# Down-projections of the prompt tokens as seven block products, their sums formed in the up stage

## The chip, the cores and the metric

The kernel runs on one core of a Trainium2 chip. A core has a matmul engine (TensorE; PE in the profile, PEld for its weight loads), three engines for element work (VectorE, DVE; ScalarE, ACT; GpSimd, POOL) and a queue engine (SyncE, SP) that issues every DMA of this kernel. The engines run side by side and wait for one another by semaphores. Each takes its instructions in a fixed order: one that waits holds up all that stand behind it. The metric is the time of one execution in microseconds (us).

## The reference

One inference step of a two-layer encoder over 1024 prompt tokens and 8 x 16 sample tokens, width 1024. Every part is computed in single precision.

```python
for l in range(2):
    h = x * (1 + sc_m) + sh_m                 # modulation from c, its own for each request
    mix = attention_l(h) @ w_o                # layer 0: own K/V; layer 1: shared K/V
    x = layer_norm(ALPHA * x + (1 + g_m) * mix)
    h = x * (1 + sc_f) + sh_f
    u = h @ w_up[l]                           # 1024 -> 5632
    y = conv_b + sum(conv_w[t] * shifted(u, t) for t in range(3))
    a, g = split(y)                           # 2816 each
    f = (gelu(g) * a) @ w_down[l]             # 2816 -> 1024
    x = layer_norm(ALPHA * x + (1 + g_f) * f)
    if l == 0:
        k_b, v_b = split((x * (1 + sc_kv) + sh_kv) @ w_kv_b)   # for layer 1
```

The outputs are x and the new K, V and convolution rows.

## The kernel before, in words

All tokens stand in nine tiles of 128: tiles 0 to 7 are the prompt, tile 8 is the sample. A matmul in this kernel reads each operand as two parts, a rounded `hi` and a rest `lo`, and is made of three: lo x hi, hi x lo, hi x hi. Cutting an operand in two is `split`: ACT casts the raw value to `hi` (`copy`, L167), then DVE or POOL subtracts it to make `lo` (L178). So a weight tile costs a DMA, a cast and a subtraction before TensorE may use it. Weights rest in rings of slots (`wslots`, four of 2 x 1024 columns); `subslots` cuts them into halves of 512 columns.

The program runs in stages, layer after layer: attention, output projection (`out_proj`), the up stage (`ffn`) and the down stage (`down`); between the layers `kv` makes layer 1's keys and values.

*Up stage.* The 22 blocks j of 128 hidden columns each have an `a` and a gate part. The first two (`plain`) are ordinary products. The other twenty (`spair`) are made as pairs, `a` block and gate block together, by seven products of half-sized blocks in place of eight (`products`): POOL forms four sums of weights of 128x512 (L1151 to L1154), ACT and DVE split each of the seven, PE does 7 x 24 matmuls of 320 or 256 columns (L1203), and ACT or DVE takes each result out of PSUM and adds it up (L1164, L1171). Then `conv_row` lays the three taps over the rows on ACT and DVE (L1289, L1250), and `gated` applies GELU on ACT, multiplies on POOL (L1297) and stores the block in `actD` (L1298). In layer 0 the modulation matmuls of the coming stages (`ada`, L224) run in the background, one step after every other product.

*Down stage.* Three groups of three tiles, GR = (0,1,2), (6,7,8), (3,4,5). In a group, for each of the 22 blocks j, `fetch` loads the whole weight block (128x1024) and the group's three activation columns (128x384) and splits both, the weights' subtraction on POOL, the activations' on DVE (L1379). `mm` then does 18 matmuls (3 tiles x 2 halves x 3, L1386) into six PSUM banks. So each weight block is loaded and split three times a layer. At a group's end `evict` multiplies the result by the gate (L1399), and `tail` adds the residual and normalizes: in layer 0 by `norm_tail`, which also transposes the rows on PE (L1016), applies layer 1's modulation (L1024 on DVE, L1028 on ACT), splits the result into `H` and stores three copies; in layer 1 by `norm_last`, which writes the output. In the last group the last KEEP blocks are held back and done tile by tile, so that the tiles end one after another.

After layer 0's last tile `kv` begins with nine value tiles (24 matmuls each, L309), then forms the sums of the normalized tiles for its own seven products (`tsums`, L1109 to L1112 and L178), then runs these.

The order of instructions on each engine is made ahead of time by a scheduler that takes the program's order as priority; `issue_after` is a written-out order.

## Time and profile before

| what | us |
|---|---|
| median of 3 runs (2810.69 to 2818.3) | 2810.72 |
| the profiled execution | 2808.31 |
| its span, first to last instruction | 2806.5 |
| matmuls of layer 0's down stage, first to last start | 1050.7 to 1335.9 |
| matmuls of layer 1's down stage, first to last start | 2515.4 to 2791.4 |
| layer 1's up stage, paired blocks | 2059.4 to 2515.3 |

The profiled execution lies 2.4 us under the median. The granted clock was 0.987 of full speed over the span. An instruction's row gives its start, its duration, its engine and line, what it writes and reads, and in brackets how long the engine had been idle and what ended that.

### The profile page before, as it was taken

To read this page: it belongs to the slowest core of one execution; us is meant where nothing else is said; L and a number is where in the kernel's file an instruction comes from. 1 tells how busy PE (TensorE), PEld (TensorE's weight loads), DVE (VectorE), ACT (ScalarE), POOL (GpSimd) and SP (SyncE) were. 2 spreads that over 40 slices of the span, in tenths; PEclk is the share of its full clock that TensorE was granted. 3 is DMA by queue.
4 is the path that set the end of the run, shared out by engine and by line. 5 is a ranking of instruction groups with operands and counts; after the bars stand their busy time and mean duration, and the time that the engine had idled before them with its cause. 6 is when DMAs were issued, how large, how long until landed. Compare 5 with 4: busy or idle time off the path is not lost.

```text
span 2806.5 us, 46569 instructions
## 1 busy us (share of the span) xinstructions
PE 2701.0 (96%) x17398; PEld 2384.3 (85%) x17398; DVE 1898.8 (68%) x3622; ACT 1307.8 (47%) x2607; POOL 1117.7 (40%) x755
## 2 busy tenths in 40 slices
...
GB/s 291 212 157 198 146 98 173 146 250 142 143 156 145 142 132 220 214 225 195 266 199 268 120 153 192 221 202 122 170 123 71 72 80 71 71 143 256 210 199 76
DMA packets 205187, 467.96 MB, mean 167 GB/s; under 512 B 34752, under 2 KB 97936, under 8 KB 204960
## 3 DMA queue, kind: packets, MB, share of 16 engines
...
q8 instruction: 137, 2.24, 0.3%
...
## 4 chain that ended last, share of the span: by engine, by line
PE 40%; DVE 4%; DMA 3%; ACT 2%; issue 1%; POOL 0%; SPq 0%; POOLq 0%; DVEq 0%; ACTq 0%
PE PS L1203 18%; PE PS L1386 10%; PE PS L296 4%; PE PS L309 4%; PE PS L590 1%; PE PS L568 1%; PE PS L540 1%; DVE F L507 1%; DMA F<-hmD 1%; PE PS L543 1%; ACT F L919 1%; PE PS L717 0%; DVE wl L178 0%; DMA F<-hD 0%; DVE xa L178 0%
## 5 line engine op out<-in xcount | busy, mean ns | idle before, releaser
L1203 PE MATMUL PS<-H,wh 128*128 128x320 f32 (+1 forms) x2752 | 427.9, 298 | 0.0
L1203 PEld LDWEIGHTS PS<-H,wh 128*128 128x128 f32 x2752 | 390.3, 192 | 0.4 <-issue 0.4
L1164 DVE TENSOR_TENSOR F<-PS,F 128x256 f32<-128x256 f32 (+1 forms) x446 | 197.7, 453 | 199.7 <-PE PS L1203 198.9
L167 ACT CAST wh<-F 128x512 fp32r<-128x512 f32 (+3 forms) x265 | 168.0, 645 | 328.3 <-PE PS L1203 186.6
L1379 DVE TENSOR_TENSOR xa<-xa 128x384 fp32r<-128x384 f32 x132 | 180.8, 1379 | 190.5 <-ACT xa L167 189.0
L1250 DVE SCALAR_TENSOR_TENSOR F<-F 128x1024 f32<-128x1024 f32 x320 | 258.9, 855 | 4.5 <-ACT F L1289 3.4
L178 DVE TENSOR_TENSOR wl<-F,wh 128x512 fp32r<-128x512 f32 (+2 forms) x236 | 215.0, 924 | 61.9 <-ACT wh L167 61.5
L1203 PE MATMUL PS<-H,wl 128*128 128x320 f32 (+1 forms) x1376 | 244.0, 300 | 8.7 <-ACT F L1171 7.2
L296 PE MATMUL PS<-H,wh 128*128 128x384 f32 (+1 forms) x1152 | 225.1, 339 | 0.0
L1386 PE MATMUL PS<-wh,xa 128*128 128x512 f32 x696 | 222.0, 395 | 0.0
L178 POOL TENSOR_TENSOR wl<-ws,wh 128x1024 fp32r<-128x1024 f32 x59 | 148.6, 2523 | 178.8 <-ACT wh L167 144.1
L1203 PEld LDWEIGHTS PS<-H,wl 128*128 128x128 f32 x1376 | 205.1, 192 | 16.9 <-ACT F L1171 7.7
L1203 PE MATMUL PS<-xa,wh 128*128 128x320 f32 (+1 forms) x1408 | 216.6, 296 | 1.4 <-DVE xa L178 1.4
L167 ACT CAST wh<-ws 128x512 fp32r<-128x512 f32 (+1 forms) x159 | 126.8, 804 | 190.8 <-PE PS L1203 94.8
L296 PEld LDWEIGHTS PS<-H,wh 128*128 128x128 f32 x1152 | 200.9, 189 | 1.3 <-issue 0.8
L1203 PEld LDWEIGHTS PS<-xa,wh 128*128 128x128 f32 x1408 | 197.4, 189 | 2.1 <-DVE xa L178 1.7
L1259 POOL TENSOR_TENSOR F<-F 128x16 f32<-128x16 f32 x88 | 47.8, 543 | 312.4 <-DVE F L1250 220.5
L1386 PEld LDWEIGHTS PS<-wh,xa 128*128 128x128 f32 x696 | 130.6, 188 | 30.7
L167 ACT CAST xa<-xa 128x384 fp32r<-128x384 f32 x132 | 67.4, 513 | 187.6 <-DMA xa<-actD 181.9
L309 PE MATMUL PS<-wh,H 128*128 128x512 f32 (+1 forms) x576 | 145.7, 367 | 1.4 <-DVE F L1095 0.8
L628 POOL TENSOR_TENSOR F<-F,X 64x512 f32<-64x512 f32 x62 | 79.5, 1282 | 169.6 <-DVE F L604 147.7
L1297 POOL TENSOR_TENSOR F<-F 128x1152 f32<-128x1152 f32 x44 | 119.8, 2722 | 49.5 <-DVE F L1250 31.3
...
## 6 DMA issues: line engine op xcount, KB each, us to landing
...
xa<-actD SPq DMA_DIRECT2D x132, 192.0 KB
...
```

Of the source, the lines that this page charges most:

```text
L167: nc.scalar.copy(out, in_)
L178: self.eng(el).tensor_sub(lo, src, hi.bitcast(F32))
L296: mm = self.nc.tensor.matmul(out[:, 0:n], w[a][:, k * 128 : k * 128 + 128], H[:, p, k, s0 : s0 + n], start=i == 0, stop=i == 23)
L309: self.nc.tensor.matmul(out[:, 0:n], H[:, p, j * kn + k, t0 : t0 + 128], w[a][:, k * n : k * n + n], start=i == 0, stop=i == 23,)
L628: self.eng("v" if last else "p").tensor_mul(on[r, q], on[r, q], rb[r, :])
L1164: nc.vector.tensor_add(d, v(ps), a if len(a.shape) == 3 else v(a))
L1203: self.pairmm = nc.tensor.matmul(ps[:, 0:m], w[a][:, k * 128 : k * 128 + 128], x(p, k, n), start=start and c == 0, stop=c == 11, skip_grou ...
L1250: nc.vector.scalar_tensor_tensor(o, u, cw[:, cc, i : i + 1], o, op0=ALU.mult, op1=ALU.add)
L1259: nc.gpsimd.tensor_add(y3[:, :, 0:2], y3[:, :, 0:2], E4[:, cc])
L1297: nc.gpsimd.tensor_mul(yg, yg, ya)
L1379: nc.vector.tensor_sub(lo, raw, hi.bitcast(F32))
L1386: self.downmm = nc.tensor.matmul(ps, a[p][:, i * 128 : i * 128 + 128], w[q][:, hf * 512 : hf * 512 + 512], start=j == 0 and c == 0, stop=j ...
```

## The change

The down-projection of the eight prompt tiles is rewritten as seven products in place of eight. The activations of a block pair m (blocks 2m and 2m+1) are cut by block and by token half into A11 (even block, tokens 0 to 511), A12 (odd, 0 to 511), A21 and A22 (tokens 512 to 1023); the weights by block and by output half into B11, B12 (even), B21, B22 (odd). The numbered products are, summed over the eleven pairs: 1 = A11 B11, 2 = A12 B21, 5 and 6 of two sums each, 3 = sum x B22, 7 = two sums, 4 = A22 x sum. Each is 128x512 by 512 columns for four token tiles: 12 matmuls a pair. The sample tile is not part of it: its matmuls ride along in products 1, 2, 5 and 6, one of 512 columns by 3 a block and half.

- The four weight sums (`weight_sums`) and four activation sums (`act_sums`) of a pair are made on POOL in the up stage, in the blocks with even j (and one at j = 3; the last activation sums fall in the down stage's third step). The weights are loaded into a buffer `w0`, summed in place and stored to `wT`; the activations are summed in place in the two gate buffers and stored to `actS`. Even blocks of `actD` are stored in part only.
- The buffer `w0` is the first of the four weight slots, so in the up stage the products have six half slots instead of eight. The `y` buffers are one for `a` and two for the gate in place of a ring of three.
- In the down stage all splits are on ACT and DVE. The weights' raw halves go through a ring or, in products 3 to 7, directly into the slot.
- Results are combined by ACT copies and DVE additions between products. The residual and the normalization of a tile are in `head`, the rest in `tail`. In layer 0 the sample tile's tail runs in product 3, those of tiles 0 to 3 in product 7, and those of 4 to 7 after product 4. `norm_rows` normalizes on ACT instead of DVE; the modulation of a transposed tile is all on ACT (VA is empty).
- `kv` has become a generator: its first value tiles (0, 1, 2, 3, 8) are issued between the last four tails.

```diff
-VA = (4, 5, 6, 7)
+VA = ()
+NK = NFF // 2
+TAILS = ({1: 8}, {0: 0, 2: 1, 5: 2, 8: 3}, {})
...
-        NW = 4
+        NW = 3
+        self.wslots = [None] + [(wh[:, i], wl[:, i]) for i in range(NW)]
...
-        ys = Ring([F[:, o : o + 1152] for o in (10492, 6396, 7548)])
+        yact = F[:, 10492:11644]
+        ygate = [F[:, o : o + 1152] for o in (6396, 7548)]
...
-            nc.sync.dma_start(self.actD[j], yg)
+            if j % 2:
+                nc.sync.dma_start(self.actD[j], yg)
+                self.pend.append(j // 2)
+            else:
+                for r in (slice(0, 512), slice(1024, 1152)):
+                    nc.sync.dma_start(self.actD[j][:, r], yg[:, r])
+
+        def act_sums():
+            for m in self.pend:
+                a11, a21 = ygate[0][:, 0:512], ygate[0][:, 512:1024]
+                a12, a22 = ygate[1][:, 0:512], ygate[1][:, 512:1024]
+                nc.gpsimd.tensor_add(a22, a21, a22)
+                nc.gpsimd.tensor_sub(a21, a11, a21)
+                nc.gpsimd.tensor_sub(a11, a22, a11)
+                nc.gpsimd.tensor_sub(a12, a12, a11)
+                for i in range(2):
+                    nc.sync.dma_start(self.actS[m, i], ygate[i][:, 0:1024])
+            self.pend = []
+
+        def weight_sums(m):
+            b11, b12, b21, b22 = (t[:, o : o + 512] for t in self.w0 for o in (0, 512))
+            for i in range(2):
+                nc.sync.dma_start(self.w0[i], I["wdn"][l, 2 * m + i])
+            nc.gpsimd.tensor_sub(b11, b12, b11)
+            nc.gpsimd.tensor_sub(b12, b22, b12)
+            nc.gpsimd.tensor_sub(b22, b22, b11)
+            nc.gpsimd.tensor_sub(b21, b22, b21)
+            for i in range(2):
+                nc.sync.dma_start(self.wT[l][m, i], self.w0[i])
...
-        sub = self.subslots(self.wslots)
+        sub = self.subslots(self.wslots[1:4])
...
             def after(i, q):
                 if i % 2 == 0:
                     self.step(1)
+                if i == 1:
+                    act_sums()
+                if i == 2 and j in wsum:
+                    weight_sums(wsum.index(j))
                 if q == 4:
-                    y.append(ys.next())
+                    y.append(ygate[j % 2])
...
+        acts = Ring([(X1[:, o : o + 640], X1[:, o + 640 : o + 1280]) for o in range(0, 8960, 1280)])
+        more = [(H[:, 0, c, 512:1024], H[:, 1, c, 512:1024]) for c in range(8)]
+        def weight(src, ring=None):
+            hi, lo = subs.next()
+            raw = ring.next() if ring else lo.bitcast(F32)
+            nc.sync.dma_start(raw, src)
+            self.split(raw, hi, lo, "a", "v")
+            return hi, lo
...
+        def product(q, banks, bs=None, new=True, keep=0, hook=None):
+            for m in range(NK - keep):
+                a, w, w2 = fetch(q, m)
+                for i in range(4):
+                    mm(self.bank(banks[i]), a, i, w, new and m == 0, m == NK - 1)
+                if bs is not None:
+                    mm(self.bank(bs), a, 4, w2, q in (1, 5) and m == 0, q in (2, 6) and m == NK - 1)
+                if hook:
+                    hook(m)
...
+        product(1, A, 4, hook=start)
+        aff = affs()
+        for i in range(4):
+            nc.scalar.copy(p1[i], self.bank(A[i]))
+        product(2, A, 4, new=False)
+        for i in range(4):
+            gate(c11[i], self.bank(A[i]), i, 0)
+        gate(cs[0], self.bank(4), 8, 0)
+        product(5, B, 4)
+        for i in range(4):
+            nc.scalar.copy(q5[i], self.bank(B[i]))
+        product(6, B, 4, new=False)
+        for i in range(4):
+            nc.vector.tensor_add(u4[i], self.bank(B[i]), p1[i])
+        gate(cs[1], self.bank(4), 8, 1)
...
+        product(3, B, new=False, hook=tails(0))
+        for i in range(4):
+            nc.vector.tensor_add(p1[i], self.bank(B[i]), p1[i])
...
+        product(7, C, hook=tails(1))
+        for i in range(4):
+            nc.vector.tensor_add(u4[i], self.bank(C[i]), u4[i])
+            nc.vector.tensor_sub(q5[i], u4[i], q5[i])
+            gate(u4[i], u4[i], 4 + i, 1)
...
+        product(4, E, keep=keep, hook=tails(2))
+        kept = [(m, fetch(4, m)) for m in range(NK - keep, NK)]
+        for i in range(4):
+            for m, (a, w, _) in kept:
+                mm(self.bank(E[i]), a, i, w, False, m == NK - 1)
+            nc.vector.tensor_sub(q5[i], q5[i], self.bank(E[i]))
+            gate(q5[i], q5[i], 4 + i, 0)
+            if l:
+                tail(4 + i)
+            else:
+                head(4 + i)
+        if not l:
...
+            self.kvrun = self.kv(*ev)
+            next(self.kvrun)
+            for i in range(4):
+                next(self.kvrun)
+                tail(4 + i)
```

292 lines of the change are left out of this document (182 added, 110 removed).

## The prediction

> **What bounds the kernel now.** The page first: its engine shares and the chain that ended last.
>
> ```profile
> span 2806.5 us, 46569 instructions
> PE 2701.0 (96%) x17398; PEld 2384.3 (85%) x17398; DVE 1898.8 (68%) x3622; ACT 1307.8 (47%) x2607; POOL 1117.7 (40%) x755
> ...
> PE 40%; DVE 4%; DMA 3%; ACT 2%; issue 1%; POOL 0%; SPq 0%; POOLq 0%; DVEq 0%; ACTq 0%
> ```
>
> PE is busy 96% of the span and is the largest share of the chain, so a matmul taken away counts in full where PE stands without a gap. Next, the source view of the down matmuls (L1386) in each layer's stretch; columns: line, engine, operation, count, duration in ns, first and last start.
>
> ```profile
> L1386 PE MATMUL PS<-wh,xa x408: 392/394/481, 1050.7 to 1335.9; 128*128 128x512 f32 x136
> ...
> L1386 PE MATMUL PS<-H,xa x540: 392/394/403, 2540.4 to 2766.3; 128*128 128x512 f32 x180
> ...
> L1386 PE MATMUL PS<-wh,xa x288: 392/394/399, 2515.4 to 2788.6; 128*128 128x512 f32 x144
> ...
> L1386 PE MATMUL PS<-xa x216: 387/389/397, 2532.2 to 2791.4; 128*128 128x512 f32 x108
> ...
> L1386 PE MATMUL PS<-wl,xa x144: 392/394/403, 2515.7 to 2788.4; 128*128 128x512 f32 x144
> ```
>
> Layer 1's four groups hold 540+288+216+144 = 1188 matmuls, started from 2515.4 to 2791.4: 276.0 us over 1187 steps, 0.2325 us each. The listed 392 ns is a latency; the spacing is what one costs. Layer 0 takes 285.2 us for as many, with 48 of its tiles' transposes between them.
>
> The third view gives busy time by stretch (PE, PEld, DVE, ACT, POOL, then clock, DMA share, GB/s): ten pairs of layer 1's up stage, the end of layer 0's, the busiest DMA stretch, and layer 1's down stage.
>
> ```profile
> 2133.54:2357.34 223.80, 223.80 (x1682) 223.80 (x1682) 172.81 (x251) 95.04 (x160) 89.65 (x70) 1.00 0.23 75
> ...
> 845.00:1045.00 200.00, 199.91 (x1548) 188.74 (x1546) 142.95 (x210) 82.61 (x137) 88.42 (x61) 1.00 0.41 135
> ...
> 1365.00:1380.00 15.00, 15.00 (x68) 12.43 (x67) 9.62 (x25) 5.47 (x13) 2.77 (x4) 1.00 1.03 399
> 2530.00:2780.00 250.00, 250.00 (x1077) 201.91 (x1076) 139.89 (x153) 103.90 (x146) 156.39 (x61) 1.00 0.61 200
> ```
>
> PE has no gap in either stage, so both are PE-bound. A pair of layer 1 lasts 22.38 us; per pair DVE is idle for (223.80-172.81)/10 = 5.1 us, POOL for 13.4.
>
> **The change, part by part.**
>
> *Fewer matmuls.* Before, 22 blocks x 9 tiles x 2 halves x 3 = 1188 a layer. After, 7 products x 11 block pairs x 4 tiles x 3 = 924, and for the sample tile 22 x 2 x 3 = 132: 1056, all of the same 512 columns. 132 fewer x 0.2325 = 30.7 us a layer, **-61.4 us** in all. All of this stands on PE's path.
>
> *Sums in the up stage.* Each block pair adds eight POOL operations of 128x512 (four on weights, four on activations), all in the even pairs: ten pairs of twenty in a layer. It also adds 3 MB of loads and stores to two pairs. These rows price them (by group; mean ns after the comma):
>
> ```profile
> L1250 DVE SCALAR_TENSOR_TENSOR F<-F 128x1024 f32<-128x1024 f32 x81 | 62.4, 812 | 0.0
> L178 DVE TENSOR_TENSOR wl<-F,wh 128x512 fp32r<-128x512 f32 x50 | 48.5, 970 | 12.0 <-ACT wh L167 12.0
> L1164 DVE TENSOR_TENSOR F<-PS,F 128x256 f32<-128x256 f32 x100 | 44.6, 454 | 36.4 <-PE PS L1203 36.4
> L178 DVE TENSOR_TENSOR wl<-ws,wh 128x512 fp32r<-128x512 f32 x20 | 27.4, 1372 | 2.6 <-ACT wh L167 2.6
> ```
>
> ```profile
> L1297 POOL TENSOR_TENSOR F<-F 128x1152 f32<-128x1152 f32 x10 | 26.9, 2692 | 15.6 <-DVE F L1250 13.8 <-DVE F L1164 1.8
> ...
> L1259 POOL TENSOR_TENSOR F<-F 128x16 f32<-128x16 f32 x20 | 7.7, 383 | 74.6 <-ACT wh L167 38.5 <-DVE F L1250 36.0
> ...
> L1151 POOL TENSOR_TENSOR F<-F 128x512 f32<-128x512 f32 x5 | 6.5, 1292 | 11.1 <-DVE wl L178 11.1
> ```
>
> Eight x 1.29 = 10.3 us, within POOL's idle 13.4. But the engines hinder each other, as the timeline of one pair shows:
>
> ```profile
> 2207.36 2.70 POOL L1297 TENSOR_TENSOR F<-F 128x1152 f32<-128x1152 f32 x1 [1.53 <-DVE F L1250]
> ...
> 2218.37 1.62 POOL L1154 TENSOR_TENSOR ws<-ws,F 128x512 f32<-128x512 f32 x1
> ```
>
> ```profile
> 2205.05 0.68 DVE L178 TENSOR_TENSOR wl<-F,wh 128x512 fp32r<-128x512 f32 x1
> ...
> 2207.86 2.74 DVE L178 TENSOR_TENSOR wl<-F,wh 128x512 fp32r<-128x512 f32 x1
> ...
> 2217.45 1.39 DVE L178 TENSOR_TENSOR wl<-F,wh 128x512 fp32r<-128x512 f32 x1 [0.23 <-ACT wh L167]
> 2218.76 0.48 DVE L1164 TENSOR_TENSOR F<-PS,F 128x320 f32<-128x320 f32 x1
> ```
>
> A split (L178) that takes 0.68 alone took 2.74 when a POOL operation had begun before it, and ended 0.54 after that one (2207.36+2.70 = 2210.06, against 2210.60); POOL's own 1.29 became 1.62 behind a split. The eviction out of PSUM stays at 0.48 beside a running POOL operation. So a DVE operation with both inputs in SBUF and a POOL operation take turns. Now this costs DVE 75.9 - 70 x 0.68 = 28 us in ten pairs, 2.8 us for 8.97 us of POOL work: 0.31 a us. Eight more at that rate cost DVE 3.2 us in an even pair, under the 5.1 idle: hidden on average. Without that cover, each waits its full 1.29: 10.3 - 5.1 = 5.2 late, x10 = 52 us in layer 1. In layer 0 the background's modulation matmuls (L224) share PE:
>
> ```profile
> 845.00:1045.00 200.00, 12.78 (x160) 3.15 (x160) 1.00 0.41 135
> ```
>
> (1548-160)/168 = 8.26 pairs in 200 us: 24.2 each, with DVE idle (200-142.95)/8.26 = 6.9. So 3.4 x 10 = 34 there. Bounds 0 and 86, for both layers. Late evictions bite first (a product is 22.38/7 = 3.2 us, and a bank is read within one), and an even pair's gate buffer must be summed and stored before its conv row may write it: ACT waits there with casts and evictions behind it. The nearest row, 0.31, gives nothing, the burst of taps something: I take 1 us an even pair in layer 1, 0.5 in layer 0: **+15 us**. SP gets seven more issues in two pairs; a store that waits for POOL holds the up-weights queued behind it, whose slots are two pairs deep. The DMA share of 0.23 to 0.41 leaves room, 65 GB/s more beside 75 to 135. Six half slots instead of eight still run 19 us ahead. All three at 0, inside the bounds.
>
> *The streams of the down stage.* Each step's splits go to ACT and DVE (in the old stage POOL took the weights'). A step of 12 matmuls is 2.8 us and needs two DVE splits, 1.4 us, so products without tails are safe; products 5 and 6 need three in 3.5 us. Product 7 carries four tiles' tails. A weight cast and one tail in layer 0 (ACT, then DVE):
>
> ```profile
> 2223.19 0.62 ACT L167 CAST wh<-ws 128x512 fp32r<-128x512 f32 x1 [1.23 <-PE PS L1203]
> ```
>
> ```profile
> 1359.82 1.51 ACT L1028 ACTIVATE F<-PS,C 128x128 f32<-128x128 f32 x4
> 1361.20 1.34 ACT L1032 COPY F<-PS 128x512 f32<-128x512 f32 x2
> 1362.44 1.06 ACT L167 CAST H<-F 128x1024 fp32r<-128x1024 f32 x1
> ```
>
> ```profile
> 1342.97 1.28 DVE L975 BATCH_NORM_STATS2 C<-F 128x6 f32<-128x512 f32 x2
> ...
> 1354.72 1.23 DVE L1040 TENSOR_TENSOR F<-F 128x1024 f32<-128x1024 f32 x1
> ```
>
> ACT now does all eight affine pieces (2 x 1.51), two copies (1.34), the cast (1.06) and the normalizing (about 1.1): 6.5, x4 = 26, and 22 casts x 0.62 = 13.6: 40 us in a product of 132 x 0.2325 = 30.7. DVE: 1.28 + 1.23 + residual 1.2, gate 0.7 and small ones 1.3, estimated by their lengths = 5.7, x4 = 23, and 22 x 0.68 = 15: 38. Both overrun, by 9 and 7; what covers it is the seven activation slots, 19.5 us of PE work whose splits (9.5 of DVE) can be done ahead. Behind it twelve operations of 0.7 form the last sums, 8.2, with no cover left. The tails' DMAs are 4 x 2 MB beside 5.8 MB of operands: 14.2 MB, 461 GB/s, where the row above is full (share 1.03) at 399: 4.9 us over. Bounds 0 and 15; I take **+5**, and +4 in layer 1, whose tails store a quarter as much.
>
> *Layer 0's end.* Before, the value tiles filled PE while three tails ran; they still do, now beside four. The one loss was here, with DVE's first operand sum, DVE's busy time (third figure) and PE's wait:
>
> ```profile
> 1368.67 0.42 DVE L1109 TENSOR_TENSOR F<-F 128x256 f32<-128x256 f32 x1 [2.83 <-DMA hmD<-F]
> ```
>
> ```profile
> 1380.00:1390.00 10.00, 10.00 (x52) 8.64 (x51) 10.00 (x28) 8.34 (x24) 0.00 (x0) 1.00 0.95 323
> 1390.00:1400.00 10.00, 8.57 (x62) 7.98 (x61) 10.00 (x34) 7.71 (x25) 0.00 (x0) 1.00 0.95 338
> ```
>
> ```profile
> 1400.84 2.50 PE L1203 MATMUL PS<-xa,wh 128*128 128x320 f32 x8 [1.39 <-DVE xa L178]
> ```
>
> PE waits for the operand sums, with DVE busy all the time. They began 32.7 us after the last down matmul (1336.0). Their target overlaps the sample gate's place, which the tails now use as a buffer to the last: five value tiles (24 x 0.23 = 5.5 each), three tiles' transposes (some 2.7), and the last tail's ACT work (4) and store (2.5) make 37. Bounds 0 and 10; I take **+4**.
>
> *Layer 1's end.* The last tile's chain:
>
> ```profile
> 2791.12 1.37 DVE L1399 TENSOR_TENSOR F<-PS,F 128x512 f32<-128x512 f32 x2 [2.57 <-PE PS L1386]
> ...
> 2797.96 1.24 ACT L997 ACTIVATE F<-F,C 128x1024 f32<-128x1024 f32 x1 [1.18 <-DVE C L996]
> 2799.28 2.34 POOL L998 TENSOR_TENSOR F<-F 128x1024 f32<-128x1024 f32 x1 [6.93 <-ACT F L997]
> 2801.65 1.23 DVE L999 TENSOR_TENSOR F<-F 128x1024 f32<-128x1024 f32 x1 [3.79 <-POOL F L998]
> ```
>
> Tile 7 ends on DVE with two operations (about 2.5) instead of 5: -2.5; but four tiles come 18 x 0.2325 = 4.2 us apart and need some 5.6 of DVE each (1.4 for the last block, 1.5 for the residual's sums, 1.5 of small ones, 1.2 for the add), up to 5 late. I take 0, bounds -3 and +3.
>
> The sum: -61.4 + 15 + 5 + 4 + 4 + 0 = -33 us, 1.2%. The profiled execution took 2808.3 (span 2806.5), the median is 2810.7: 2808.3 - 33 = 2775, by the median 2778.
>
> **The rivals.**
> 1. *The turns fill up* (slower). The eight sums land in the bursts of taps, even pairs run late, PE waits for evictions. It decides where the mean loss of the 20 even pairs passes (61.4-13)/20 = 2.4 us. At the full bound: -61.4+13+86 = +38, 2848; halfway past the point, 2825. For it: 2.74 for 0.68. Against: 0.31 us a us, and DVE's idle time.
> 2. *Each takes its turn for its whole length.* Per pair DVE's paired-input work is 6.2 + 70 x 0.68/10 = 11.0, POOL's 5.2+2.7+0.8 = 8.6; two pairs and the sums 2 x 19.6 + 10.3 = 49.5, against 44.8 of PE in layer 1 and 48.4 in layer 0: 47 + 11 = 58 us lost, -61.4+58+13 = +10: 2820. Against it: a split ends 0.54 behind POOL's end, not 0.68, so the turns are shorter than the rows. The Trainium skill, SBUF — State Buffer, "Who interferes with whom", states this rule: a vector instruction with two SBUF inputs and a GpSimd one that reads SBUF exclude each other, the first to issue keeping the port for its whole instruction. The trace agrees on the exclusion and not quite on its length.
> 3. *Everything is hidden*: nothing but the matmuls, -61+3: 2752. For it: PE without a gap in both stages today.
> 4. *The tails choke the down stage*: SP waits on tails' stores with fetches behind, products 7 and 4 lose 15 us a layer: -61.4+15+30 = -16: 2794.
>
> **How the numbers follow.** Forecast 0.36; rival 1 0.24; 2 0.12 (half of it within 0.3%, which is 8 us and about what a measurement can tell); 3 0.13; 4 0.15 (0.02 of it within). Faster 0.36+0.13+0.13 = 0.62, same 0.08, slower 0.30. The range reaches down past rival 3, to 2750, and up to 2838, leaving out the worse half of rival 1. The likeliest case alone: 2762 to 2795.
>
> **What would show it.** Down matmuls: 1056 a layer, 0.2325 apart, near 246 us. Up stage: DVE's mean split above 1.08, pairs alternately long and short; wrong if an even pair passes 22.38 + 2.4. Waits of PE in products 7 and 4 beyond 10 us a layer would prove the fourth rival, and a first operand sum later than 40 us the step at layer 0's end.

## The result, and the profile after

The changed kernel takes 2850.36 us (median of four runs, 2845.37 to 2852.07), the kernel before beside it 2813.33: a ratio of 1.0132, with a 95% interval of 1.0113 to 1.0150. It is 1.3% slower; forecast were 2778 us and 1.2% faster. The profiled execution took 2852.07 us, 43.8 more than that of before, at a mean granted clock of 0.971 (before 0.987).

The page after, its span, PE's share and the chain that ended last:

```profile
span 2850.0 us, 47209 instructions
...
PE 2682.3 (94%) x17134; PEld 2359.3 (83%) x17134; DVE 2030.9 (71%) x3850; ACT 1347.1 (47%) x2752; POOL 1109.9 (39%) x808
...
PE 16%; DVE 2%; DMA 2%; issue 1%; ACT 0%; SPq 0%; DVEq 0%; ACTq 0%
```

PE has 264 matmuls fewer, yet it is busy only 19 us less where 61 were to go, because it runs at a lower clock for a part of the time (2701.0 - 61.4 = 2639.6, times 0.987/0.971, is 2683); and it is idle 62 us longer (43.5 of span and 18.7 of its own). DVE has 132 us more of busy time. The source view of the down matmuls in layer 1 shows that the saving itself was made:

```profile
L1465 PE MATMUL PS<-wh,xa x584: 389/394/793, 2570.0 to 2825.9; 128*128 128x512 f32 x195
...
L1465 PE MATMUL PS<-wl,xa x292: 392/399/628, 2571.5 to 2825.6; 128*128 128x512 f32 x146
...
L1465 PE MATMUL PS<-H,xa x180: 389/394/399, 2754.0 to 2829.4; 128*128 128x512 f32 x180
```

584 + 292 + 180 = 1056, as forecast; they take 259.4 us, where 0.2325 apart would be 245.3 (1055 steps). By stage, from the starts of the first and last matmul of each (us; "V" is from the first value tile to the first product of layer 1's keys and values, "kv" those products, "attention" from there to layer 1's first paired block):

| kernel | up, layer 0 | down, layer 0 | V | kv | attention | up, layer 1 | down, layer 1 | after the last matmul | span |
|---|---|---|---|---|---|---|---|---|---|
| before | 508.7 | 285.2 | 51.7 | 96.5 | 575.0 | 456.0 | 275.9 | 15.2 | 2806.5 |
| after | 527.9 | 270.7 | 56.3 | 107.2 | 576.8 | 487.6 | 259.3 | 20.6 | 2850.0 |
| difference | +19.2 | -14.5 | +4.6 | +10.7 | +1.8 | +31.6 | -16.6 | +5.4 | +43.5 |

The up stages lose 50.8 us, and the down stages keep only 31.1 of their 61.4. Where the up stage loses, the windows view shows (length, then busy time of PE, PEld, DVE, ACT, POOL with counts, then granted clock, DMA share, GB/s): the first five pairs of layer 0 are the first row, ten late ones the second; the other three are layer 1's first and second pair and its last fourteen.

```profile
542.91:668.38 125.47, 107.70 (x801) 99.12 (x801) 88.41 (x123) 43.32 (x76) 93.36 (x68) 0.90 0.84 298
...
750.11:1003.69 253.58, 253.32 (x1992) 232.89 (x1989) 176.33 (x261) 98.77 (x165) 138.51 (x99) 1.00 0.49 165
...
2082.01:2117.21 35.20, 25.45 (x169) 25.01 (x170) 30.33 (x49) 14.80 (x29) 30.96 (x25) 0.85 0.69 238
2117.21:2142.33 25.12, 22.81 (x171) 22.35 (x170) 24.44 (x26) 9.15 (x16) 23.09 (x15) 1.00 0.55 188
...
2255.43:2569.62 314.19, 313.90 (x2354) 313.41 (x2352) 268.95 (x353) 133.51 (x229) 175.35 (x120) 1.00 0.29 101
```

The last fourteen pairs of layer 1 take 314.19 / 14 = 22.44 us each, though every second has its four activation sums: those cost nothing. The whole loss stands in the first pairs, which last 35.2, 25.1, 30.1, 28.7, 26.9 and 27.5 (before: 29.6 and then 22.4), with DVE and POOL busy nearly throughout. The source view of the first weight sum says why:

```profile
L1347 POOL TENSOR_TENSOR w0f<-w0f x11: 1288/1737/3177, 2064.8 to 2237.2; 128x512 f32<-128x512 f32 x11
```

All eleven weight sums of layer 1 start within 172 us, one in every pair and some pairs with two, instead of one in every second pair over 440. They depend on nothing but their buffer and their loads, so the scheduler puts them as early as the buffer allows, whatever block of the program they are written in. Groups of DVE, each of one shape, and then of POOL in these six pairs (2082 to 2255 us; busy time, mean ns, idle before):

```profile
L1276 DVE SCALAR_TENSOR_TENSOR F<-F 128x1024 f32<-128x1024 f32 x21 | 41.4, 1973 | 0.9 <-ACT F L1315 0.9
L188 DVE TENSOR_TENSOR wl<-F,wh 128x512 fp32r<-128x512 f32 x31 | 45.4, 1469 | 7.1 <-ACT wh L177 6.0 <-issue 0.9
```

```profile
L1348 POOL TENSOR_TENSOR w0f<-w0f 128x512 f32<-128x512 f32 x10 | 18.7, 1866 | 3.7 <-DMA w0f<-in_wdn_dram 3.7
...
L1350 POOL TENSOR_TENSOR w0f<-w0f 128x512 f32<-128x512 f32 x10 | 14.7, 1473 | 0.4
```

The kernel before has, for the same tap of 1024 columns in ten pairs of this stage (the row of the prediction, 812 ns, mixes it with short ones):

```profile
L1250 DVE SCALAR_TENSOR_TENSOR F<-F 128x1024 f32<-128x1024 f32 x41 | 52.4, 1278 | 0.0
```

A split takes 1469 ns in place of 970, a tap of 1024 columns 1973 in place of 1278: beside POOL operations both are longer. PE's waits in the up stage of layer 1 (time, count, longest) then fall on the evictions that stand behind those on DVE and ACT:

```profile
PE PS L1228 <- DVE F L1189: 19.3, 10, 4.8
...
PE PS L1228 <- ACT F L1196: 7.7, 1, 7.7
```

### The profile page after: what moved, and what is told of

Same layout as the page of the kernel before. It is cut to its first block, busy times and chain, and to the rows that moved or that the text cites. A ratio compares the mean times of both kernels' runs of the same rounds, so it can differ in the third digit from the quotient of the medians.

```text
span 2850.0 us, 47209 instructions
## 1 busy us (share of the span) xinstructions
PE 2682.3 (94%) x17134; PEld 2359.3 (83%) x17134; DVE 2030.9 (71%) x3850; ACT 1347.1 (47%) x2752; POOL 1109.9 (39%) x808
## 5 line engine op out<-in xcount | busy, mean ns | idle before, releaser
L1228 PE MATMUL PS<-H,wh 128*128 128x256 f32 (+1 forms) x2624 | 408.9, 298 | 0.0
L1465 PE MATMUL PS<-wh,xa 128*128 128x512 f32 x1144 | 370.2, 402 | 14.8 <-DVE F L1583 5.8
L1228 PEld LDWEIGHTS PS<-H,wh 128*128 128x128 f32 x2624 | 373.6, 192 | 0.0
L1276 DVE SCALAR_TENSOR_TENSOR F<-F 128x1024 f32<-128x1024 f32 x320 | 309.6, 1014 | 27.8 <-ACT F L1315 27.6
L1189 DVE TENSOR_TENSOR F<-PS,F 128x320 f32<-128x320 f32 (+1 forms) x446 | 196.5, 451 | 126.4 <-PE PS L1228 124.4
L188 DVE TENSOR_TENSOR wl<-F,wh 128x512 fp32r<-128x512 f32 (+2 forms) x234 | 245.0, 1056 | 57.4 <-ACT wh L177 55.3
L177 ACT CAST wh<-F 128x512 fp32r<-128x512 f32 (+2 forms) x234 | 137.2, 595 | 314.0 <-PE PS L1228 191.8
L1228 PE MATMUL PS<-H,wl 128*128 128x256 f32 (+1 forms) x1312 | 234.3, 301 | 21.2 <-ACT F L1196 15.2
L1465 PE MATMUL PS<-wl,xa 128*128 128x512 f32 x572 | 229.0, 401 | 0.2
L188 DVE TENSOR_TENSOR xa<-xa 128x640 fp32r<-128x640 f32 (+1 forms) x154 | 124.0, 810 | 119.5 <-ACT xa L177 111.6
L177 ACT CAST xa<-xa 128x640 fp32r<-128x640 f32 (+1 forms) x154 | 104.1, 682 | 169.4 <-DMA xa<-actD 109.5
L188 DVE TENSOR_TENSOR wl<-ws,wh 128x512 fp32r<-128x512 f32 (+1 forms) x149 | 156.1, 1052 | 10.2 <-ACT wh L177 10.2
L1315 ACT ACTIVATE F<-F 128x1152 f32<-128x1152 f32 x80 | 108.0, 1351 | 115.8 <-DVE F L1189 60.1
L1228 PE MATMUL PS<-xa,wl 128*128 128x320 f32 (+1 forms) x664 | 123.4, 308 | 20.8 <-DVE F L1189 20.0
## 6 DMA issues: line engine op xcount, KB each, us to landing
xa<-actS SPq DMA_DIRECT2D x88, 256.0 KB
```

The lines of the kernel that those rows point to most:

```text
L177: nc.scalar.copy(out, in_)
L188: self.eng(el).tensor_sub(lo, src, hi.bitcast(F32))
L1189: nc.vector.tensor_add(d, v(ps), a if len(a.shape) == 3 else v(a))
L1228: self.pairmm = nc.tensor.matmul(ps[:, 0:m], w[a][:, k * 128 : k * 128 + 128], x(p, k, n), start=start and c == 0, stop=c == 11, skip_grou ...
L1276: nc.vector.scalar_tensor_tensor(o, u, cw[:, cc, i : i + 1], o, op0=ALU.mult, op1=ALU.add)
L1315: nc.scalar.activation(y, u[:, 2:1154], AF.Identity, bias=cw[:, cc, 3:4], scale=cw[:, cc, 2:3])
```

## The experiments

The theory at the start: rival 1, made worse by the bunching; the turns of POOL and DVE are the loss, so sums that are spread, moved or left out give it back. Its rival: the loss comes from what lies around the sums, the DMA traffic, one buffer less, the waits in the down stage and the tails. Each ratio is against the kernel before in runs on the same chip; the four without an interval are of one run each. The stages come from one profiled execution of each.

| run | median, us | before there | ratio (95%) |
|---|---|---|---|
| e1_spread_even | 2825.45 | 2806.22 | 1.0068 (1.0046 to 1.0091) |
| e2_spread_odd | 2838.61 | 2806.22 | 1.0107 (1.0083 to 1.0131) |
| e3_no_weight_adds | 2812.00 | 2806.22 | 1.0021 |
| e4_h_split_dve | 2856.52 | 2806.22 | 1.0179 |
| e5_three_places | 2822.55 | 2802.30 | 1.0069 (1.0048 to 1.0091) |
| e6_adds_on_vector | 2840.38 | 2802.30 | 1.0140 (1.0119 to 1.0160) |
| e7_sums_in_layer0 | 2843.10 | 2803.82 | 1.0130 (1.0106 to 1.0154) |
| e8_rows_on_vector | 2843.27 | 2803.82 | 1.0139 (1.0106 to 1.0172) |
| e9_one_per_pair | 2830.09 | 2807.53 | 1.0090 (1.0073 to 1.0107) |
| e10_scale_on_vector | 2823.01 | 2805.21 | 1.0063 |
| e11_tails_first | 2819.19 | 2805.21 | 1.0050 |
| e12_sums_in_attention | 2844.18 | 2806.86 | 1.0136 (1.0115 to 1.0158) |
| e13_one_per_head | 2823.93 | 2806.61 | 1.0057 (1.0043 to 1.0072) |
| e14_three_splits | 2818.24 | 2806.61 | 1.0051 (1.0030 to 1.0072) |
| e15_best_places | 2818.81 | 2804.46 | 1.0059 (1.0038 to 1.0081) |
| e16_copies_first | 2799.97 | 2805.45 | 0.9977 (0.9964 to 0.9990) |

Their stages, as above:

| kernel | up, layer 0 | down, layer 0 | V | kv | attention | up, layer 1 | down, layer 1 | after the last matmul | span |
|---|---|---|---|---|---|---|---|---|---|
| e1 | 520.6 | 264.8 | 56.3 | 107.5 | 574.6 | 477.9 | 257.2 | 21.4 | 2821.9 |
| e2 | 522.2 | 264.6 | 56.1 | 106.9 | 576.2 | 480.9 | 256.5 | 20.3 | 2837.8 |
| e3 | 522.0 | 263.3 | 56.2 | 107.4 | 575.5 | 464.5 | 256.7 | 18.9 | 2810.2 |
| e4 | 528.1 | 259.4 | 63.2 | 111.3 | 580.6 | 489.6 | 255.7 | 19.6 | 2854.6 |
| e5 | 517.2 | 264.5 | 59.7 | 102.6 | 578.5 | 480.1 | 256.0 | 19.4 | 2823.0 |
| e6 | 523.4 | 263.1 | 67.3 | 104.1 | 576.0 | 484.4 | 258.6 | 18.6 | 2835.4 |
| e7 | 549.7 | 265.8 | 62.0 | 111.7 | 575.6 | 460.7 | 260.9 | 18.7 | 2848.6 |
| e8 | 551.7 | 263.5 | 63.5 | 108.0 | 578.5 | 461.4 | 258.4 | 17.3 | 2842.3 |
| e9 | 527.3 | 264.8 | 61.8 | 106.1 | 579.6 | 468.1 | 259.2 | 18.5 | 2824.3 |
| e10 | 520.8 | 264.8 | 56.5 | 104.7 | 578.2 | 474.6 | 257.5 | 19.2 | 2821.2 |
| e11 | 521.1 | 267.3 | 54.5 | 103.9 | 577.2 | 475.0 | 255.8 | 19.8 | 2817.4 |
| e12 | 513.5 | 266.1 | 54.5 | 103.2 | 616.1 | 461.2 | 258.9 | 17.4 | 2829.3 |
| e13 | 512.7 | 269.4 | 54.5 | 103.2 | 601.9 | 461.2 | 257.0 | 16.8 | 2819.7 |
| e14 | 513.1 | 264.2 | 61.6 | 105.7 | 596.4 | 461.3 | 257.9 | 16.4 | 2816.1 |
| e15 | 513.4 | 270.0 | 54.5 | 104.6 | 576.2 | 474.5 | 262.7 | 18.2 | 2815.9 |
| e16 | 516.1 | 262.5 | 54.5 | 103.6 | 577.7 | 477.2 | 252.4 | 17.2 | 2807.1 |

### The weight sums' place and their turns

**e1_spread_even** holds the sums' loads behind the up weights of their pair, and their POOL operations behind the last gated product:

```diff
-            for i in range(2):
-                nc.sync.dma_start(self.w0[i], I["wdn"][l, 2 * m + i])
-            nc.gpsimd.tensor_sub(b11, b12, b11)
+            with self.tc.issue_after(self.wupdma):
+                for i in range(2):
+                    nc.sync.dma_start(self.w0[i], I["wdn"][l, 2 * m + i])
+            with self.tc.issue_after(self.gmul):
+                nc.gpsimd.tensor_sub(b11, b12, b11)
...
```

> The weight sums are tied to their pair: the loads behind that pair's up-weights, the four POOL operations behind the gate product of the pair before; eight sums then stand in each even pair, as the prediction had assumed, and the amount of work is the same. Theory A (the loss of the up stages, 19 and 32 us, comes from the weight sums standing bunched in the first pairs): both stages come back to 2 us a pair or less over the kernel before, 508.7+10 and 456+10 at most, and the whole to 2800 to 2822. Rival B (POOL's added work costs its turns wherever it stands): both stages stay where they are, 528 and 488, and the whole at 2840 to 2855.

**e2_spread_odd** does the same in pair 2 and the odd pairs, where no activation sums stand:

```diff
-        wsum = [2, 3] + list(range(4, NFF - 1, 2))
+        wsum = [2] + list(range(3, NFF, 2))
```

> As the run before, but the weight sums stand in the odd pairs and the activation sums in the even ones: four added POOL operations in each pair. Theory A: the stages within 3 us of the kernel before (512 and 459), the whole 2798 to 2810. Rival B: no change, 2840 to 2855. If the eight in one pair are a cost of their own, this run is 10 us or more under the one with eight in even pairs; if not, the two agree within 4 us.

**e3_no_weight_adds** keeps the loads and stores, bunched as in the changed kernel:

```diff
-            nc.gpsimd.tensor_sub(b11, b12, b11)
-            nc.gpsimd.tensor_sub(b12, b22, b12)
-            nc.gpsimd.tensor_sub(b22, b22, b11)
-            nc.gpsimd.tensor_sub(b21, b22, b21)
```

> The four POOL operations of the weight sums are left out (the products then take the plain weights, so the output is another); the loads of the down weights and the stores stay bunched at the stage's start. Theory A: the stages lose their POOL part, 509 to 515 and 456 to 462, the whole 2798 to 2812. Rival C (the transfers, or the queue that issues them, hold up the up weights): the stages stay near 528 and 488, the whole 2840 or more.

Without the 88 operations of the weight sums the kernel stands 0.2% above before instead of 1.3%: they are most of the loss. What is left of the up stage's loss in e3 (13.3 and 8.5 us) stands in the first four pairs. In layer 0 the sums' loads and stores crowd there (below); in layer 1 some 5 us remain even in e7 and e12, which have none of them in that stage. Spreading the sums gives back a little more than half of their cost. The source view of e1 in layer 1, and two of its neighbouring pairs in the windows view:

```profile
L1349 POOL TENSOR_TENSOR w0f<-w0f x11: 1721/1742/1754, 2086.3 to 2506.3; 128x512 f32<-128x512 f32 x11
```

```profile
2191.09:2214.91 23.82, 22.64 (x171) 22.37 (x170) 21.83 (x26) 10.50 (x17) 15.12 (x12) 1.00 0.39 127
2214.91:2237.28 22.37, 22.37 (x171) 22.37 (x169) 20.39 (x25) 8.15 (x15) 18.00 (x12) 1.00 0.40 142
```

and one of the kernel before:

```profile
2200.00:2222.40 22.40, 22.40 (x171) 22.40 (x170) 17.28 (x26) 9.51 (x16) 8.97 (x7) 1.00 0.24 74
```

Spread, one weight sum costs a pair of layer 1 1.4 us; in layer 0 the pairs behind the first three stay at 25.1 to 25.4, as before, until the background ends. For two pairs POOL's listed time grows by 15.12 + 18.00 - 2 x 8.97 = 15.2 us and DVE's by 21.83 + 20.39 - 2 x 17.28 = 7.7: half a microsecond a microsecond, where the prediction carried over 0.31. The pair with both kinds of sums leaves DVE 2 us idle in 23.8, and its evictions come late. In the odd pairs (e2) it is no better: there nearly every pair of layer 1 takes 22.9 or 23.4, and 5.7 us pass between layer 0's up and down stage.

**e5_three_places** is e1 with layer 0's sums moved away from the stage's first pairs (and two edits for the layer's end, below):

```diff
+        wsum = [2, 3] + list(range(4, NFF - 1, 2)) if l else list(range(6, NFF - 1, 2)) + [11, 15, 19]
```

> The kernel with the weight sums spread over the even pairs, and three edits in three separate stages. (1) Layer 0's weight sums start four pairs later (pairs 6, 8 ... 20 and 11, 15, 19), so that none lies beside the sixteen 384 KB copies of the skew table in pairs 2 to 4. If these copies and the sums' transfers crowd each other out, pair 3 of layer 0 (34.9 us when spread) falls to 29 to 31 us and layer 0's products from 520.6 to 510 to 515 us. If it is the activation sums or the six half slots, pair 3 stays at 33 us or more, the products at 518 us or more. (2) At layer 0's end the norm tails of tiles 4 to 7 use another second buffer, so that the operand sums' region is no longer held by the last stores of h. If that region makes them late, the first operand sum comes 36 to 41 us after the last down matmul (48 now), the first key/value pair takes 27 to 31 us (37.7) and V tiles to first product 51 to 54 us (56.3). If the amount of VectorE and GpSimd work is the limit, they stay at 44, 35 and 55 us or more. (3) In layer 1's last four tiles VectorE makes scale and shift for all four (GpSimd had them for two). If GpSimd's long multiplications block VectorE there, the time from last matmul to end falls from 21.4 to 16 to 18.5 us; if VectorE's own backlog is the limit, it is 21 to 24 us. Together by the first theories 2800 to 2808 us, ratio 0.997 to 1.001; by the others 2822 to 2828 us.

**e6_adds_on_vector** puts the weight sums of e5 on DVE (and, in the down stage, holds back casts and splits and takes the residual part of the tails of tiles 8 and 0 to 3 to DVE, as e7 to e9 also do; below):

```diff
-            with self.tc.issue_after(self.gmul):
-                nc.gpsimd.tensor_sub(b11, b12, b11)
+            nc.vector.tensor_sub(b11, b12, b11)
...
```

> As the kernel with three edits, and four more. (1) The four operations of each weight sum run on VectorE, not GpSimd. VectorE was busy 17.3 us of a pair's 22.4 us before, so 4 x 0.68 = 2.7 us more fit: if the sums cost by the taking of turns, even pairs of layer 1 go from 23.8 to 22.4 to 22.8 us and its products from 478 to 461 to 468 us. If VectorE's total is the limit, they stay at 23.5 and 474 us or more. (2) ScalarE's casts of product 2 from its fourth block on stand behind the copies of product 1's sums, VectorE's splits of product 3 likewise behind the additions after product 6. If the order on these queues makes the boundary stalls, each boundary loses under 1 us (4 to 5 us now): 6 to 8 us less in each down stage. If the banks themselves must be emptied first, 2 us or more stay at each. (3) The norm tails of tiles 8 and 0 to 3 make their residual split on VectorE, those of 4 to 7 on GpSimd as now. By turns, layer 0's products 3, 7 and 4 lose 6 to 10 us less (264.8 us for the stage becomes 248 to 254 with the boundaries), and the V tiles don't pay for it (the run with all nine on VectorE paid 7 us there). If VectorE's total is the limit, the stage stays at 257 us or more. (4) Seven blocks, not six, are kept for layer 1's last tiles: 1 to 2 us less behind the last matmul if a backlog is left there, none if not. Together by the first theories 2760 to 2778 us, ratio 0.983 to 0.989; by the others 2800 us or more.

In both a spare buffer of the last tails lies over the row that scales the normalized rows of layer 0's tiles 4 to 7, so that these rows, which are layer 1's residual, are other numbers; the instructions are the same. Layer 0's second pair (j = 3) in the windows view, in e1 and then in e5:

```profile
572.32:607.18 34.86, 25.52 (x204) 23.27 (x200) 26.33 (x34) 12.11 (x21) 19.11 (x14) 0.96 1.00 369
```

```profile
576.66:604.04 27.38, 25.50 (x204) 23.23 (x201) 16.94 (x26) 8.42 (x15) 8.98 (x8) 1.00 0.97 350
```

The DMA engines are full here in both. A sum in this pair costs 7.5 us, where one in the pairs from 6 to 18 costs nothing (the one in pair 20, behind the background, costs 3.5). In e3, which has the sums' loads and stores here but none of their operations, the pair takes 36.7 us:

```profile
579.60:616.30 36.70, 25.64 (x202) 23.30 (x201) 24.13 (x34) 12.09 (x20) 16.40 (x11) 0.94 1.01 357
```

At this one place it is the transfers, which the prediction had put at nothing. On DVE the sums cost layer 1 4.3 us more than on POOL (484.4 against 480.1, one profile of each): DVE does not take them for less. ACT was not tried.

**e7_sums_in_layer0** puts all 22 weight sums in layer 0's up stage, two in each even pair from 6 to 18 and one in each odd pair from 5 on, where the background matmuls give each pair 3 us more:

```diff
+        wsum = {}
+        if l == 0:
+            for n, j in enumerate(range(6, 20, 2)):
+                wsum[j, 2], wsum[j, 5] = (0, n), (1, n)
+            for n, j in enumerate((5, 7, 9, 11, 13, 15, 17, 19)):
+                wsum[j, 2] = (n % 2, 7 + n // 2)
```

> All 22 weight sums, layer 1's too, are formed in layer 0's up stage (pairs 5 to 19, one in an odd pair, two in an even one), where a pair lasts 25.4 us because background matmuls lie in it and where a spread sum has cost nothing so far. Layer 1's up stage forms activation sums alone. Beside it: at layer 0's end tiles 4 to 7 use a second buffer for h that no operand sum and no normalisation row needs; tiles 8 and 0 to 3 split on VectorE; layer 1's last four tiles scale and shift on VectorE, with seven blocks kept. Theory: the price of a weight sum is the price of the pair it lies in. Then layer 0's pairs stay at 25.1 to 25.8 us and its products at 515 to 521 us (two sums a pair fit), layer 1's products fall from 478 to 458 to 464 us (456.0 before), layer 0's down stage takes 255 to 258 us, the first key/value pair 29 to 34 us with the first operand sum 38 to 43 us after the last down matmul, the last stretch 18 to 19 us. Sum: 2780 to 2796 us beside 2802 to 2807 of the kernel before, ratio 0.991 to 0.998. Rival: a sum costs 1.4 us wherever it lies as soon as GpSimd is full; then layer 0's even pairs take 27 to 29 us, its products 530 us or more, and the whole is 2800 us or more. If the activation sums or the six half slots cost in layer 1, its products stay above 468 us.

**e9_one_per_pair** does at most one in a pair, eleven and four in layer 0 and seven in layer 1:

```diff
+        if l == 0:
+            wsum = {j: (0, j - 5) if j < 16 else (1, j - 16) for j in range(5, 20)}
+        else:
+            wsum = {j: (1, 4 + n) for n, j in enumerate((4, 6, 8, 10, 12, 14, 16))}
```

> From the kernel with the sums spread over even pairs. (1) One weight sum in each of layer 0's pairs 5 to 19 (its own eleven, four of layer 1), the other seven of layer 1 in even pairs of its own up stage. Theory: a pair of layer 0 takes one sum free, not two. Its pairs 5 to 19 stay at 25.1 to 25.8 us, its products at 514 to 521 us, layer 1's at 466 to 472 us (seven at 1.4 us on 461). Rival: odd pairs have no room beside the activation sums; then 525 us or more. (2) Gate, normalisation and first residual rows are loaded in products 2 and 5, not at product 1's end, where transfers kept the DMA engines 91 to 98% busy. If that makes the stall between products 1 and 2, product 2 takes 38.5 to 39.5 us in both layers (43 to 46 in most runs); if it is the copies' place on ScalarE's queue, 42 or more. VectorE's splits of product 3 from its third block on stand behind the additions after product 6: product 6 falls from 44 to 46 us to 39 to 42 if their order is the cause. (3) In tiles 4 to 7 of layer 0 VectorE makes four of the eight scalings of h, as before the change; among the V tiles ScalarE was 84 to 93% busy, VectorE 19 to 38%. If ScalarE is the limit there, V tiles to first product take 52 to 54.5 us (56.3), the first key/value pair 28 to 34 (37.7); if not, 56 and 37 or more. Tiles 8 and 0 to 3 split on VectorE; layer 1's end as in the last runs (17 to 19 us). Together 2776 to 2792 us beside 2802 to 2807, ratio 0.989 to 0.996; by the rivals 2805 us or more.

Nineteen pairs of layer 1 in e7, in the windows view:

```profile
2139.57:2568.84 429.27, 427.11 (x3193) 425.43 (x3192) 364.71 (x478) 180.47 (x309) 237.10 (x164) 1.00 0.27 96
```

22.6 us each, with the activation sums still there: without weight sums layer 1's up stage loses 4.7 us instead of 31.6, which shows their cost by itself. But layer 0 pays more than that (549.7, 41 above before): its pairs in which the operations of two sums ran go up to 31.1 (its profiled execution is the highest of its six). One in every pair (e9) still lengthens some of them, up to 27.8; one in about every second pair (e5) does not.

**e12_sums_in_attention** moves layer 1's weight sums into its attention, and **e13_one_per_head** puts each behind the bias load of a head, with six buffers for the probabilities in place of four, but one weight slot for q in place of two:

```diff
+            if l and 6 <= i < 50 and i % 4 == 2:
+                self.next_weight_sums(i // 4 - 1)
             scores(x)
```

> The kernel with tails first, and layer 1's eleven weight sums formed during layer 1's attention, where GpSimd is busy 6 to 12 us of 50 and the DMA engines 42 to 77%; their buffer is the weight slot w0, for which attention's two weight slots move up by one and two of its six buffers for transposed probabilities go. Layer 0's sums in its pairs 5 to 19, eleven of them; layer 1's end as in the last runs. Theory: the sums cost by the turns that they force on VectorE in a stage where it has no slack, so in attention they cost nothing: layer 1's products take 459 to 463 us (475.0 with tails first, 456.0 before the change), the stretch from the last key/value product to layer 1's first product 575 to 580 us (577.2), layer 0's products 515 to 519 us, the last stretch 18 to 19 us. Together 2794 to 2802 us beside 2802 to 2807 of the kernel before, ratio 0.995 to 0.999. Rival: attention has no room either (the two buffers less, or the turns beside its softmax); then the stretch takes 590 us or more and the whole 2812 us or more.

```diff
-        for i in range(2):
-            nc.sync.dma_start(w[i], self.I["wdn"][1, 2 * m + i])
+        with self.tc.issue_after(self.biasdma):
+            for i in range(2):
+                nc.sync.dma_start(w[i], self.I["wdn"][1, 2 * m + i])
```

> As the run with layer 1's weight sums in attention, but one sum behind the bias load of each of eleven heads (they ran there all eleven in the first 170 us, with the DMA engines 76 to 92% busy), and with all six buffers for transposed probabilities (that run had four, which fall to be written again before they are read, so that its attention's numbers are others) and one weight slot for q. Theory: bunching is again what cost 39 us there; spread, the sums cost nothing in a stage in which GpSimd and the DMA engines have room: the stretch from the last key/value product to layer 1's first product 575 to 584 us (577.2 with the sums in the up stage, 616.1 bunched), layer 1's products 459 to 463 us, layer 0's 512 to 516 us; together 2786 to 2800 us beside 2802 to 2807 of the kernel before, ratio 0.992 to 0.999. Rival: GpSimd's turns cost VectorE in attention as well, or the single q slot does; then the stretch takes 590 us or more and the whole 2808 us or more.

In e12 the four buffers are overwritten before they are read, so that layer 1's attention computes other numbers; its profiled execution is the lowest of its five. PE's waits in the attention of e13:

```profile
PE PS L551 <- DVE C L518: 7.0, 7, 4.8
...
PE PS L601 <- DVE C L736: 6.9, 1, 6.9
```

The same 50 us of layer 1's attention in e11, without the sums, and in e12 (windows):

```profile
1550.00:1600.00 50.00, 45.44 (x280) 40.74 (x279) 32.04 (x97) 32.50 (x76) 10.10 (x14) 1.00 0.42 117
```

```profile
1550.00:1600.00 50.00, 46.06 (x261) 39.73 (x260) 30.40 (x91) 30.37 (x70) 22.12 (x20) 0.95 0.76 222
```

POOL is mostly free there (10.10 of 50 us), but PE waits for small results of DVE, and beside the sums it gets through 261 matmuls in place of 280. Against e11 attention is 39 us longer with bunched sums, 25 with one a head. But turns between POOL and DVE are not what these traces show. The sums of e13 run at their short length, and DVE is listed as busy for 391.2 us of its attention, against 390.4 in e11. The wait of 6.9 us above goes back to ACT, which stood for 8.5 us at a cast into the sums' buffer until a store of the sums had left it:

```profile
L1089 POOL TENSOR_TENSOR w0f<-w0f x11: 1282/1287/1297, 1542.0 to 1777.8; 128x512 f32<-128x512 f32 x11
```

```profile
1788.88 1.04 ACT L177 CAST w0r<-ws 128x1024 fp32r<-128x1024 f32 x1 [8.54 <-DMA wT<-w0f]
```

The wait of 4.8 us goes back, over DVE and POOL, to the load of a head's bias. So the buffer, q's one slot and the transfers (DMA share 0.67 in e13's attention, 0.59 in e11's) are left as causes here, and which of them makes how much of the 25 us stays open. Nothing tried makes the sums free in layer 1.

### Layer 0's end

**e4_h_split_dve** takes the residual part of the transposed tiles from POOL to DVE in all nine tails of layer 0:

```diff
-EL = "p"
+EL = "v"
```

> The changed kernel with the subtraction that splits a normalized tile in layer 0's down stage on DVE instead of POOL, nothing else. If the turns between the engines cost layer 0's last products and the first pair of the key products (39.5 us in product 4 against 30.7, 37.1 in the key pair against 27.0), the two lose 3 to 10 us together and the whole is 2840 to 2847; if DVE's own amount of work is the limit there, it is the same or slower, 2850 to 2856.

Product 4 of layer 0 in the windows view, in the changed kernel and in e14, which does so for four tiles (8, 0, 1 and 2):

```profile
1302.00:1341.50 39.50, 35.28 (x156) 28.05 (x155) 37.69 (x45) 24.44 (x53) 22.00 (x7) 0.96 0.63 227
```

```profile
1283.70:1316.30 32.60, 32.54 (x148) 26.04 (x147) 32.15 (x43) 20.80 (x42) 10.73 (x3) 1.00 0.74 262
```

With these splits on POOL, DVE is busy 37.69 of 39.50 us and product 4 is 7 us longer. Off POOL that is gone, but the value tiles behind it pay the same (63.2 and 61.6 us in place of 56.3 and 54.5). **e14_three_splits** is e13 with that edit; it is not to be told from e13 (1.0051 against 1.0057).

> As the run with one sum per head, and the residual split of tiles 8, 0, 1 and 2 (not 3 to 7) on VectorE. GpSimd's split of 2.4 us and its turns cost layer 0's product 4 some 7 us (39.5 us against 32.4 in each run that had tiles 8 and 0 to 3 on VectorE), but there the V tiles paid 5 us. If tile 3's split alone, the last before the V tiles, made them pay, product 4 takes 33 to 36 us and the V tiles stay at 54 to 55.5 us: 3 to 6 us less than that run, 2782 to 2796 us, ratio 0.990 to 0.998. If every operation more on VectorE before the V tiles is paid there, the V tiles take 57 us or more and the whole is the same within 2 us.

The first 40 us behind the last down matmul, and where the operand sums of the next products begin (windows; timeline):

```profile
1341.50:1381.50 40.00, 39.11 (x185) 31.98 (x185) 25.00 (x53) 26.46 (x52) 17.06 (x7) 1.00 0.68 258
...
1384.96 1.26 DVE L1065 TENSOR_TENSOR F<-F 128x1024 f32<-128x1024 f32 x1 [4.70 <-POOL F L1064]
...
1389.69 1.09 DVE L1134 TENSOR_TENSOR F<-F 128x256 f32<-128x256 f32 x3 [2.50 <-DMA hD<-F]
```

The kernel before has, in the same place:

```profile
1335.90:1375.90 40.00, 40.00 (x190) 33.35 (x189) 27.92 (x51) 16.91 (x35) 15.97 (x11) 1.00 0.64 236
```

The first sum comes at 1389.7 - 1341.5 = 48.2 us (before 32.7; forecast 37), and PE's first pair of products behind it takes 37.1 us in place of 27.0. No engine is full here: each tail goes from ACT to DVE to POOL and back, and the engines wait for one another, as DVE's 4.70 us for a multiplication on POOL show. Is it the buffer over which the sums are formed, as the prediction had it? e5 frees it, by its second edit:

```diff
+            rings = Ring([zt]), Ring([self.hf, self.lng])
```

```profile
L1134 DVE TENSOR_TENSOR F<-F x9: 399/413/1880, 1334.6 to 1403.1; 128x256 f32<-128x256 f32 x9
```

The sums then begin at 8.3 us behind the last down matmul, but those of the last tile at 76.8 (76.5 in the changed kernel): the last tile is the limit, and not the buffer. (e7 and e8 free it as well, with another spare buffer, and begin at 13 us.) **e8_rows_on_vector** is e7 with the residual's multiplication of tiles 4 to 7 on DVE, **e10_scale_on_vector** is e1 with half of the scalings of these tiles on DVE (and five buffers more for raw weights), **e11_tails_first** is e1 with each tail ahead of a value tile:

```diff
-                self.norm_tail(t, row, xdst, aff, True, tb, "a", "pv", None, ...
+                self.norm_tail(t, row, xdst, aff, True, tb, "a", "vv" if t in (4, 5, 6, 7) else "pv", None, ...
```

> As the run with all weight sums in layer 0's up stage, and in the norm tails of tiles 4 to 7 of layer 0 the multiplication of the residual row by the scale row (1024 elements, about 2.6 us on GpSimd) is VectorE's. If VectorE, idle for some 30 us of the V tiles, waits there for GpSimd, the stretch from the V tiles to the first product and the first key/value pair lose 2 to 6 us less together. If VectorE's amount of work is the limit (four more operations of 1.2 us), they lose 2 to 5 us more, as with the split on VectorE (7 and 4 us more). The other stages stay within 1 us of that run.

```diff
-        early = Ring(raws + [F[:, o : o + 512] for o in (0, 512, 1024)])
+        early = Ring(raws + [F[:, o : o + 512] for o in range(0, 4096, 512)])
...
-                self.norm_tail(t, ..., rings[1], EL, VA, self.hD, True)
+                self.norm_tail(t, ..., rings[1], EL, (4, 5, 6, 7) if t in (4, 5, 6, 7) else VA, self.hD, True)
```

> The kernel with the sums spread over even pairs, with two edits alone. (1) At layer 0's end, for tiles 4 to 7 only, VectorE makes four of the eight scalings of h (ScalarE makes all eight in the kernel of the change); the residual split stays on GpSimd. ScalarE is busy 37.9 of the 40 us after the last down matmul there (25.5 before the change), VectorE 28.0. If ScalarE's amount of work is what delays the operand sums, the last of them ends 66 to 72 us after the last down matmul (76.8), the first product starts at 53 to 55 (56.5) and the first key/value pair takes 28 to 33 us (37.7). If VectorE is the limit, as the two runs say that gave it the split or the rows, they come at 77 or more, 56.5 or more and 37 or more. (2) The ring of raw weight halves for products 1 and 2 has fourteen buffers instead of nine, so that the load queue does not stand still until VectorE has split an old one (it stood 6.7 us in product 1). If that standstill makes the stall between products 1 and 2, product 2 takes 38.5 to 39.5 us in both layers (39.3 and 42.5 in the spread kernel, 43.0 and 43.0 in the kernel of the change); if not, layer 1's stays above 42.

```diff
             for i in range(4):
-                next(self.kvrun)
                 tail(4 + i)
+                next(self.kvrun)
```

> The kernel with the sums spread over even pairs; at layer 0's end the norm tail of tiles 4 to 7 stands ahead of a V tile in TensorE's order and not behind it, so that each tile's transposes come some 5.5 us earlier, and the chain transposes, eight scalings, two copies, cast and store with them. If the order (GpSimd waited 12.6 us for the first transposes) makes the operand sums late, the last operand sum comes 71 to 73 us after the last down matmul (76.8) and the first pair takes 32 to 34 us (37.7). If the norms before the transposes are late anyway, TensorE waits for them: the V tiles take 2 to 6 us more, 58 to 62 us, and the last sum stays at 76 or more.

The expectation of e10 counts overlapping instructions twice: the row above has ACT at 26.46 us of 40, not 37.9. Moving its scalings gives 2.8 us in kv, and the sums start no earlier (48.0). e8 is e7 within their intervals. The order of the tails (e11) gives 1.8 in V and 3.6 in kv, and e12, e13, e15 and e16, which have it too, keep that. The rest, some 10 us, was not removed by anything tried here.

### The products of the down stage

From the starts of their matmuls, each product in the changed kernel (us; 165 matmuls 0.2325 apart are 38.4, 132 are 30.7; layer 0 has transposes besides):

| product | 1 | 2 | 5 | 6 | 3 | 7 | 4 |
|---|---|---|---|---|---|---|---|
| layer 0 | 39.0 | 43.0 | 38.5 | 44.5 | 34.5 | 31.7 | 39.5 |
| layer 1 | 39.2 | 43.0 | 38.7 | 44.6 | 32.4 | 30.8 | 30.6 |

The fourth rival's products, 7 and 4, lose nothing in layer 1. Products 2 and 6 lose 4.6 and 6 us in both layers. Product 6 loses about half of them at its end, where PE waits 2.8 us in layer 0 (first row) and 3.0 in layer 1 for the first addition that empties its banks. At the start of product 2 in layer 0 the waits, the timeline and the windows view show:

```profile
PE PS L1465 <- DVE F L1583: 2.8, 1, 2.8
PE PS L1465 <- DVE xa L188: 2.7, 1, 2.7
```

```profile
1113.21 0.72 ACT L177 CAST xa<-xa 128x640 fp32r<-128x640 f32 x1 [7.26 <-DMA xa<-actD]
```

```profile
1111.00:1114.70 3.70, 1.15 (x5) 0.57 (x4) 0.74 (x1) 1.49 (x3) 0.00 (x0) 1.00 1.00 356
1115.57:1118.98 3.41, 3.41 (x10) 2.64 (x9) 2.05 (x3) 3.18 (x6) 0.00 (x0) 0.50 0.46 139
```

ACT stands for 7.26 us before a cast that waits for its load. Behind that cast on its queue stand the four copies that empty product 1's banks, into which product 2 must write; PE idles for 2.55 us and soon after runs 3.41 us at half the clock, which together cost 2.55 + 3.41 x 0.5 = 4.3 of the 4.6 us. The profile has PE's wait end with DVE's split behind that cast (2.7 us, and 2.9 in layer 1), so in the changed kernel the late load ends it, with the copies just behind. Two theories: the transfers are too late (e9 moves three groups of other loads out of the way, e10 has a deeper ring), or the copies stand in the wrong place on ACT's queue. Neither of the transfers' edits helps by itself: product 2 takes 47.7 and 44.4 us in the two layers of e9 and 40.8 and 42.3 in e10, against 39.3 and 42.5 in e1. (It varies: without any edit to it, it takes 38.5 and 40.0 in e5.) **e15_best_places** gathers the best places so far: e11, e12's places in layer 0, the loads moved as in e9, the ring of e10.

> The cheapest places found, in one kernel: layer 0's weight sums as in the last two runs (its products 513 us), layer 1's in the even pairs of its own up stage (475), tails first (V tiles 54.5, key/value stage 103.5), layer 1's end on VectorE (17 to 18.5), all splits of the tails on GpSimd. By these rows: 2817.4 - 8 - 2 = 2807 us. New in it are two edits of product 1's transfers together, which did not help one by one: gate, normalisation and residual rows are loaded in products 2 and 5, and fourteen raw buffers instead of nine keep the load queue from standing. If bytes and a standing queue together make the stall between products 1 and 2, product 2 takes 38.5 to 39.5 us in both layers (40.1 to 47.7 in the runs before) and the whole is 2796 to 2802 us beside 2802 to 2807, ratio 0.996 to 1.000. If the copies' place on ScalarE's queue or the latency of the small sample loads makes it, product 2 stays at 40 us or more and the whole at 2804 to 2812 us.

Product 2 takes 43.1 and 44.4 us there, and now PE waits for the copies (2.8 us in layer 0, first row; 3.8 in layer 1). The timeline in layer 1, just ahead of product 2:

```profile
PE PS L1467 <- ACT x2f L1579: 2.8, 1, 2.8
```

```profile
2580.59 0.72 ACT L177 CAST xa<-xa 128x640 fp32r<-128x640 f32 x1 [3.84 <-DMA xa<-actD]
2581.22 1.55 ACT L1579 COPY x2f<-PS 128x512 f32<-128x512 f32 x3
```

In e6 the order was tried for product 2. In layer 0 it took 38.5 us, but product 5 then 42.5; in layer 1 the copies stood behind the residual's scaling, which waits for its own load:

```profile
2602.24 1.06 ACT L1533 ACTIVATE F<-F 128x1024 f32<-128x1024 f32 x1 [8.20 <-DMA F<-xd]
2603.20 2.03 ACT L1577 COPY x2f<-PS 128x512 f32<-128x512 f32 x4
```

**e16_copies_first** is e15 with the order alone changed: from the fourth block on, the casts of products 2 and 6 are issued behind the copies, and so is layer 1's scaling.

```diff
             for m in range(NK - keep):
-                a, w, w2 = fetch(q, m)
+                with ExitStack() as es:
+                    if hold is not None and m > 2:
+                        es.enter_context(self.tc.issue_after(hold))
+                    a, w, w2 = fetch(q, m)
...
-            nc.scalar.copy(p1[i], self.bank(A[i]))
-        product(2, A, 4, new=False, hook=later(self.ln_gates))
+            hold = nc.scalar.copy(p1[i], self.bank(A[i])).ins
+        product(2, A, 4, new=False, hook=later(self.ln_gates), hold=hold)
```

> As the run with the best places, and on ScalarE's queue the casts of products 2 and 6 from their fourth block on, and layer 1's scaling of the residual rows, stand behind the copies of the product before. In that run TensorE waited 3.0 and 3.8 us for these copies at the start of product 2, and ScalarE stood before them at a cast that waited 3.8 us for its load; in an earlier run with the casts held back layer 0 lost nothing there, and layer 1 still 4.2 us, since the scaling of a residual row waited 8.2 us for its load in front of the copies. If the place on ScalarE's queue is what makes this stall, product 2 takes 38.5 to 39.5 us in both layers (43.1 and 44.4) and the whole is 2804 to 2811 us, ratio 1.000 to 1.004. If late loads make it whatever the order is, the waits turn into waits for casts of product 2's first blocks, product 2 stays at 42 us or more, and the whole at 2813 to 2820 us.

Product 2 in e16, layer 0 and layer 1, in the windows view:

```profile
1099.80:1138.30 38.50, 38.50 (x167) 30.97 (x166) 19.57 (x28) 16.22 (x27) 0.00 (x0) 1.00 0.58 188
...
2576.30:2614.80 38.50, 38.50 (x166) 30.97 (x166) 19.75 (x28) 15.52 (x26) 0.00 (x0) 1.00 0.58 191
```

No gap is left in either. e16 takes 2799.97 us (2792.56 to 2809.14, twelve runs), 0.9977 of before (0.9964 to 0.9990): faster than before by a quarter of a per cent, and the only version here that is. Its profiled execution is the highest of the twelve, so its stages are to be read for their inside and not for their sum. The two down stages take 514.9 us in it, 532.7 in e15 and 522.0 in e1: so a part of the gain over e15 may only undo what e15's other edits had cost. Whether the order would do without them was not tried. Product 2 alone is 4.6 and 5.9 us of the 18.8 between e15 and e16. Product 6 still takes 43.4 and 42.8, and with the splits of product 3 held back behind its additions it took 42.6 to 45.6 (e6, e9); which of its neighbours delays it, the additions of its result, tile 8's normalization or the casts for product 3, stays open.

### Layer 1's end

The changed kernel's last rows (timeline):

```profile
2831.34 5.11 POOL L1016 TENSOR_TENSOR x2f<-x2f,F 128x1024 f32<-128x1024 f32 x2 [37.87 <-ACT x2f L1015]
...
2832.12 2.14 DVE L1513 TENSOR_TENSOR F<-F 128x512 f32<-128x512 f32 x1
2834.24 3.29 DVE L1011 SCALAR_TENSOR_TENSOR F<-F,C 128x1024 f32<-128x1024 f32 x1
...
2845.03 1.28 DVE L1012 SCALAR_TENSOR_TENSOR F<-F,C 128x1024 f32<-128x1024 f32 x1
```

Two multiplications on POOL hold DVE's gate (2.14 us) and residual (3.29, against 1.28 for its neighbour of the same size): turns again, where the prediction had counted DVE's work alone. e6 to e9 and e12 to e16 have them on DVE and hold back seven blocks instead of six:

```diff
-VT = (0, 3, 6, 7)
+VT = (0, 3, 4, 5, 6, 7)
...
-KEEP = (4, 6)
+KEEP = (4, 7)
```

The end then takes 16.4 to 18.7 us, in place of 20.6 (18.9 to 21.4 in the seven versions without either edit; e5, with the first alone, 19.4; before, 15.2).

## Why the prediction was wrong

By its own terms, in the profiled executions:

| term | forecast | measured |
|---|---|---|
| 264 matmuls fewer, at 0.2325 | -61.4 | -61.4 |
| sums in the up stage | +15 | +50.8 |
| streams of the down stage, stalls | +9 | +30.3 |
| layer 0's end (V and kv) | +4 | +15.3 |
| layer 1's end | 0 | +5.4 |
| the rest (start, gaps, attention) | 0 | +3.1 |
| sum | -33 | +43.5 |

The stalls are 270.7 - 245.3 - 9.2 (what transposes add in layer 0, by the kernel before) and 259.4 - 245.3.

*The step that failed is the sums in the up stage*, twice over; it is 36 of the 77 us between the forecast and the measured sum, and the down stage's stalls are 21, the two ends 17. The prediction took the sums for what the code seems to say, "all in the even pairs", and so priced a mean load of eight POOL operations in two pairs; the weight sums went to the front, two or three times as dense, and that is 17 of the 51 us (e1). And it priced them at 0.31 us of DVE time a microsecond of POOL's and let the idle 5.1 us cover it; the measured rate is 0.5, and idle time on the mean did not cover it: 1.4 us an even pair of layer 1 when spread (the guess had been 1). Its bounds of 0 and 86 held. It also put the transfers at nothing, and in layer 0's second pair they cost 7.5 us. Rival 1 is what happened in this stage, with the place named for it wrong: not the bursts of taps in each even pair, but the first six pairs. That it gave 2848 at its full bound, and 2850.4 was measured, is luck: the sums cost 50.8 and not 86, which with the prediction's other terms would be 2810.7 - 61.4 + 50.8 + 13 = 2813, and the rest came from the terms below. (Half of its +38 is 2830, and not 2825.)

*Rival 2* had each operation hold the ports for its whole length, 4.7 us lost for each two pairs of layer 1; spread over the stage (e1) it is 1.4, so the turns are shorter than the listed lengths, as the split that ended 0.54 behind POOL had said. The Trainium skill, SBUF — State Buffer, "Who interferes with whom", states the exclusion, and this trace agrees: beside the sums splits go from 970 to 1469 ns, and without one side (e3) 1.1 of the 1.3% are gone. *Rival 3*, all hidden, fell with the first pairs. *Rival 4* fell as stated: product 7 loses nothing, product 4 loses 7 us in layer 0 to POOL's splits and not to the fetches' queue on SP.

*The down stage's streams.* Products 7 and 4 were taken to be the ones at risk; the stalls stand mostly in 2 and 6 (21 of the 30 us), at the boundaries behind 1 and 6 above all. The prediction had counted ACT's and DVE's work in a product and not the order and the late loads at its edge. Behind 1, four bank copies queue on ACT behind casts that wait for loads; in e15 that order is the cause (e16 takes 4.6 and 5.9 us away), while in the changed kernel the load itself came last. Behind 6, PE waits for DVE's first addition, and the cause stays open.

*Layer 0's end* had the right place and its first operand sum was later than the 40 us named as the test, at 48. Its mechanism, the buffer under the sums, is not the limit (e5); the rows point to the chain of the four last tails over three engines, where the order of the tails gave back 5 us; the rest stays open. *Layer 1's end* lay outside its bounds of -3 and +3; two rows show POOL's turns there.

What the prediction asked to see, it got in part: 1056 matmuls a layer, but in 259.4 us of layer 1 and not 246; splits at 1469 ns in the first six pairs, above 1080; pairs above 24.8 us, its own sign for being wrong, though not the even ones alone; a first operand sum behind 40 us.
